# A four-layer decoder trunk on one core: input sums of the FFN spaced out, pairs begin with the unsummed blocks, the norm's matmuls five rounds later

## Chip, core and metric

One core of a Trainium2 chip (trn2). The metric is the device time of one execution in microseconds, here of the one core that runs. Engines: PE is TensorE, DVE is VectorE, ACT is ScalarE, POOL is GpSimd, SP is SyncE, which issues most of the transfers.

## The reference

Four layers on x of shape (1, 512, 1024), each a token mixer and an FFN, both with a norm in front and a residual. All data is float32. The change concerns the FFN:

```python
def rms_norm(x, g):
    return x * rsqrt(mean(x * x, axis=-1) + 1e-6) * g

def conv_ffn(h, w_up, conv_w, conv_b, w_down):      # h: (512, 1024)
    gu = h @ w_up                                   # (512, 5632)
    gate, up = gu[..., :2816], gu[..., 2816:]
    gp = pad(gate, two rows in front)
    conv = conv_b + conv_w[2] * gate + conv_w[0] * gp[0:512] + conv_w[1] * gp[1:513]
    return (silu(conv) * up) @ w_down               # (512, 1024)

for i in range(4):
    x = x + mixer_i(rms_norm(x, norm_mix[i]))
    x = x + conv_ffn(rms_norm(x, norm_ffn[i]), f_w_up[i], f_conv_w[i], f_conv_b[i], f_w_down[i])
```

## The kernel before

**Layout.** x stands transposed: eight tiles x0 to x7 of 128 features by 512 tokens. Every float32 operand of a large product is split in two parts of a shorter type, a high part (written by ACT) and a low part (the rest, written by DVE), and a product is three matmuls: high by high, high by low, low by high (`mm3`, all at L302). A weight tile arrives by DMA as `wraw` or `fraw`, is split into `wh` (ACT, L239) and `wl` (DVE, L242), and there are three buffers of each, so a split is set off when TensorE has finished with an earlier tile (`freew`).

**The end of a mixer.** The output projection of a mixer ends with `x_in` for each of the eight tiles: DVE adds the bank to x (L452), ACT writes `xh`, x times the norm's gain, and the square, DVE writes `xl` (L463) and adds the square to `acc` (L466). When all eight are in, `norm_task` sums `acc` over the partitions with eight small matmuls (`av<-ones,acc`), takes the inverse root on DVE and ACT, and, ahead of an FFN, spreads it with four transposes (L521) and a copy (L523) to `sbc`, which multiplies the FFN's products afterwards.

**The FFN.** 22 blocks of 128 hidden features, each with a gate and an up product. The first two blocks are plain: `plain(0)` and `plain(1)` make gate0, up0, gate1, up1 with 24 matmuls each of 512 columns (`fm`). Their banks are in the rings "a" (three banks) and "lg" (two banks), and are given back when DVE has multiplied them by `sbc` (L670). The other 20 blocks go in ten pairs. A pair is a two by two block product in Winograd's form: seven products of 24 matmuls with 256 columns (`product`) in place of eight. It needs sums of the input's blocks, which `combine(j)` makes once in an FFN from x tiles j and j + 4, for j = 0 to 3: ACT writes y (L623), DVE q1, t3, q2, t4 (L627, L628, L631, L632) into an "r" buffer, ACT splits off `ch` (L293) and DVE `cl` (L295). It also needs sums of the weights' blocks: s1 and s3 come from a load and a second, adding transfer issued by POOL (L256), s2 and s4 from additions on POOL (L220). After a block's two products, `post` does the convolution, the silu, the product with up, and the split into `hh` and `hl` (L646 to L661). The "r" ring has three buffers; `combine`, `plain_post` and the pairs take from it.

**Order.** The program is emitted by generators: TensorE's products are the main line, and after each step of three matmuls of `fm`, or two steps of `product`, a `round` lets every spawned task go on to its next `yield`. What is emitted earlier has the higher priority. A planner in the framework then orders each engine's queue by that priority and by when it expects operands to be ready, and places buffers. On the chip every engine works its queue in order.

Of the kernel before, what the change touches and what calls it, by code (L numbers as in the profile page):

```python
# [25 lines left out]
PARTS = ((0, 4), (4, 8), (8, 12), (12, 16), (16, 22))  # L26

PLAIN = 2
LAM_INIT = 0.8 - 0.6 * math.exp(-0.3 * 2)


# [64 lines left out]
class Builder:  # L96
# [402 lines left out]
    def norm_task(self, bcast):  # L499

        nc = self.nc
        while self.nacc < KD:
            yield
        self.log_exp()
        b = yield from self.take("av")
        for c in range(4):
            self.mm(b[:, 2 * c:2 * c + 2], self.acc[:, c * 128:(c + 1) * 128], self.ones, c == 0, c == 3)
        n = 4
        yield
        u, t, rs, e2 = (self.st[:, 8 * i:8 * i + n] for i in range(4))  # L510
        nc.vector.tensor_scalar(u, b[:, 0:2 * n:2], 1.0 / D, EPS, op0=OP.mult, op1=OP.add)
        self.give("av")
        yield
        yield from self.rsqrt(rs, u, t)
        nc.vector.tensor_scalar(e2, u, EPS, None, op0=OP.mult)
        self.rs, self.e2 = rs, e2
        if bcast:
            yield
            b = yield from self.take("av")
            for c in range(4):  # L520
                nc.tensor.transpose(b[:, c * 128:(c + 1) * 128], rs[:, c:c + 1].to_broadcast([128, 128]), self.ident)  # L521
            yield
            nc.scalar.activation(self.sbc_t, b, AF.Copy)  # L523
            self.give("av")
            self.sbc = self.sbc_t
# [51 lines left out]
    def ffn_weights(self, l):  # L577
        for p, (f0, f1) in enumerate(PARTS):
            downs = 0
            for f in range(f0, f1, 2):  # L580
                t = [self.ap["wup"][(l * NF + f) * 2 + i] for i in range(4)]
                if f < PLAIN:
                    for a in t:
                        self.add_item(self.add_load(a, 1024))
                    continue
                w11 = self.add_load(t[2], 1024)
                s1 = self.add_load(t[0], 1024, "fraw", t[1])
                s2 = self.add_sum(s1, w11)
                s3 = self.add_load(t[0], 1024, "fraw", t[2])
                w12 = self.add_load(t[3], 1024)  # L590
                s4 = self.add_sum(w12, s2)
                w22 = None
                for i, s in enumerate((w11, s1, s2, w12, s3, s4, w22)):
                    self.add_item(s or self.add_load(t[1], 1024))
                    if i in (4, 6) and p and downs < 4:
                        self.add_weights(f"wd{p - 1}", (l * 4 + downs,), 1024)
                        downs += 1
        self.add_weights(f"wd{p}", range(l * KD, (l + 1) * KD), 128 * (f1 - f0))

    def ffn(self, l):  # L600
# [14 lines left out]

        def combine(j):

            while self.xver[j] != stage or self.xver[j + 4] != stage:
                yield
            y = yield from self.take("cv")  # L620
            c = yield from self.take("r")
            c = c.rearrange("p a b -> p (a b)")
            nc.scalar.activation(y, self.x[j], AF.Copy, scale=self.cols[:, gain + j:gain + j + 1])  # L623
            yield
            q1, t3, q2, t4 = (half(c, i) for i in range(4))
            x, k = self.x[j + 4], j + 4
            nc.vector.tensor_tensor(q1, half(y, 0), half(y, 1), op=OP.subtract)  # L627
            nc.vector.scalar_tensor_tensor(t3, half(x, 1), self.cols[:, gain + k:gain + k + 1], half(y, 1), op0=OP.mult,  # L628
                                           op1=OP.subtract)
            yield  # L630
            nc.vector.scalar_tensor_tensor(q2, t3, -1.0, half(y, 0), op0=OP.mult, op1=OP.subtract)  # L631
            nc.vector.scalar_tensor_tensor(t4, half(x, 0), ng[:, k:k + 1], q2, op0=OP.mult, op1=OP.subtract)  # L632
            self.give("cv")
            yield
            h, lo = (fp.tile([128, 1024], F32R, name=f"c{n}{j}") for n in "hl")
            yield from self.split(h, lo, c)
            self.give("r")
            comb[j] = h, lo
# [36 lines left out]
        def plain(f):  # L675
            state = {}
            self.spawn(plain_post(f, state))
            for name, tag in (("gate", "a"), ("up", "lg")):
                w, b = self.getw(), self.now(tag)
                self.fm(b, w, self.xsrc, range(KD))  # L680
                self.freew()
                state[name] = b

        def block(a, b):

            return lambda j: tuple(half(t, b) for t in self.xsrc(j + 4 * a))

        def csrc(i):
            def f(j):
                self.until(lambda: j in comb)  # L690
                return tuple(half(t, i) for t in comb[j])
            return f

        def product(out, src, first=False):

            w = self.getw()
            for j in range(4):
                b = src(j)
                for i in range(2):
                    sl = slice((4 * i + j) * 128, (4 * i + j + 1) * 128)  # L700
                    self.mm3(half(out, i), (w[0][:, sl], w[1][:, sl]), b, first and i + j == 0, True)
                if j % 2:
                    self.round()
            self.freew()
# [6 lines left out]
        def pair(f, downs):  # L711
            st = {}

            def between():
                for _ in range(2):
                    next(downs, None)

            def keep(name, bank):
                st[name] = yield from copied(bank)

            def a_left(bank):
                while "s" not in st:
                    yield
                st["ra"] = yield from self.take("r")
                nc.vector.tensor_tensor(st["ra"][:, :, :256], gu(st["s"]), gu(bank), op=OP.add)
                self.give("a", "cp")

            def a_right(bank):
                while "d" not in st or "ra" not in st:
                    yield  # L730
                nc.vector.tensor_tensor(st["ra"][:, :, 256:], gu(st["d"]), gu(bank), op=OP.add)
                self.give("lg", "cp")
                yield
                yield from scaled(f, st["ra"])

            def b_right(bank):
                while "n" not in st:
                    yield
                st["rb"] = yield from self.take("r")
                nc.vector.scalar_tensor_tensor(st["rb"][:, :, 256:], gu(bank), -1.0, gu(st["n"]), op0=OP.mult,  # L740
                                               op1=OP.subtract)
                self.give("cp")
                st["b"] = True

            def b_left(bank):
                nc.scalar.activation(st["rb"][:, :, :256], gu(bank), AF.Copy, scale=-1.0)
                self.give("a")
                yield
                yield from scaled(f + 1, st["rb"])

            def scaled(f, r):
                nc.vector.tensor_tensor(r, r, self.sbc[:, None, :].to_broadcast([128, 2, S]), op=OP.mult)
                yield
                yield from post(f, r)

            A = self.now("a")
            product(A, block(0, 0), True)
            self.spawn(keep("s", A))
            C = self.now("lg")
            product(C, csrc(0), True)  # L760
            self.spawn(keep("n", C))
            self.until(lambda: "s" in st)
            product(A, csrc(2))
            self.spawn(keep("d", A))
            B = self.now("a")
            product(B, block(1, 0), True)
            self.spawn(a_left(B))
            self.until(lambda: "d" in st)
            product(A, csrc(1))
            self.spawn(b_right(A))  # L770
            between()
            self.until(lambda: "n" in st)
            product(C, block(1, 1))
            self.spawn(a_right(C))
            self.until(lambda: "b" in st)
            product(A, csrc(3))
            self.spawn(b_left(A))
            between()
# [2 lines left out]
            self.until(lambda: f in hid)  # L781
            return hid[f]

        for j in range(4):
            self.spawn(combine(j))
        def downs(f0, f1):

            for _ in self.down_steps(hsrc, range(f0, f1), self.x_add, per=2):
# [3 lines left out]
        d = iter(())  # L792
        for p, (f0, f1) in enumerate(PARTS):
# [7 lines left out]
            d = downs(f0, f1)  # L801
# [1125 lines left out]
```

## Time and profile before

| what | us |
|---|---|
| median of 3 runs | 2389.44 |
| lowest, highest | 2388.29, 2394.17 |
| the profiled execution | 2390.37 |
| its span, first to last instruction | 2388.6 |
| TensorE busy | 2331.5 |
| VectorE busy | 1769.0 |
| ScalarE busy | 1280.5 |
| GpSimd busy | 315.4 |

The profiled execution is 0.9 us above the median, and 1.8 us of it lie outside its span. The mean granted clock of TensorE over the span is 0.991 of full speed. The FFNs' beginnings lie at about 313, 898, 1517 and 2027 us.

### The profile page before, as it was taken

How to read it: one execution, taken by the hardware profiler on the slowest of the kernel's cores; microseconds unless marked ns; L12 is line 12 of the kernel's file. 1: busy time of each engine (PE TensorE's matmuls, PEld its weight loads, DVE VectorE, ACT ScalarE, POOL GpSimd, SP SyncE). 2: the span in 40 equal slices, each digit the busy share in tenths (PEclk: the TensorE clock that was granted, in tenths of full speed). 3: DMA queues.
4: the chain of work that ended last, by engine and by line, in shares of the span. 5: the costliest groups of instructions: out<-in, count | busy, mean ns of one | idle time of the engine just before them, and what ended most of it. 6: DMA issues, size and time to landing. Idle time of an engine off the chain costs nothing.

```text
span 2388.6 us, 41006 instructions
## 1 busy us (share of the span) xinstructions
PE 2331.5 (98%) x16116; PEld 2115.6 (89%) x16116; DVE 1769.0 (74%) x3152; ACT 1280.5 (54%) x2378; POOL 315.4 (13%) x242
## 2 busy tenths in 40 slices
PE   8999989999999999999999998899999999999999
PEld 8999969999997768999989997799999987899998
DVE  6565688787768759877786666798777686987775
ACT  5555555444557756544454554464445575644443
POOL 0000022122002102222100000222220000222220
PEclk9999999999999999999999999999999999999999
DMA  5232255554221126555425454455552442655532
GB/s 181 82 98 89 89 141 164 154 150 133 78 93 45 34 65 173 159 154 151 120 94 159 133 137 113 141 162 150 148 149 76 139 108 91 173 159 158 155 115 84
DMA packets 98160, 298.43 MB, mean 125 GB/s; under 512 B 12144, under 2 KB 18480, under 8 KB 97968
## 3 DMA queue, kind: packets, MB, share of 16 engines
q1 hardware_dynamic: 85296, 249.67, 32.9%
q0 software_dynamic: 12672, 46.14, 11.0%
q8 instruction: 127, 2.08, 0.4%
q14 instruction: 65, 0.53, 0.1%
HBM read 273.62 MB, written 4.32 MB: 116 GB/s over the span
## 4 chain that ended last, share of the span: by engine, by line
PE 93%; DVE 3%; ACT 2%; DMA 1%; issue 1%; SPq 0%; POOL 0%; DVEq 0%; ACTq 0%; POOLq 0%
PE a L302 49%; PE tr L302 19%; PE lg L302 17%; PE av L302 3%; PE tr L961 2%; PE tr L863 2%; DVE r L628 1%; ACT wh L239 0%; DMA sk<-ql 0%; DVE wl L242 0%; DMA sk<-qh 0%; ACT xh L456 0%; DVE acc L466 0%; DMA x<-in_x_dram 0%; DVE xl L463 0%
## 5 line engine op out<-in xcount | busy, mean ns | idle before, releaser
L239 ACT ACTIVATE wh<-wraw 128x1024 fp32r<-128x1024 f32 (+3 forms) x357 | 358.0, 1008 | 493.6 <-PE a L302 216.5
L242 DVE TENSOR_TENSOR wl<-wraw,wh 128x1024 fp32r<-128x1024 f32 (+3 forms) x357 | 441.6, 1239 | 150.9 <-ACT wh L239 149.9
L302 PE MATMUL a<-wh,xh 128*128 128x256 f32 (+1 forms) x1088 | 315.0, 290 | 6.3 <-ACT xh L456 6.3
L302 PE MATMUL a<-wl,xh 128*128 128x256 f32 (+1 forms) x1088 | 311.7, 287 | 0.0
L302 PE MATMUL a<-wh,xl 128*128 128x256 f32 (+1 forms) x1088 | 311.0, 287 | 0.3 <-DVE xl L463 0.3
L302 PE MATMUL a<-ch,wh 128*128 128x256 f32 x960 | 271.7, 283 | 0.0
L302 PE MATMUL a<-cl,wh 128*128 128x256 f32 x960 | 271.5, 283 | 0.0
L302 PE MATMUL a<-ch,wl 128*128 128x256 f32 x960 | 271.4, 283 | 0.0
L302 PE MATMUL tr<-hl,wh 128*128 128x512 f32 x656 | 256.1, 390 | 0.0
L302 PE MATMUL tr<-hh,wh 128*128 128x512 f32 x656 | 255.7, 392 | 0.0
L302 PE MATMUL tr<-hh,wl 128*128 128x512 f32 x656 | 250.5, 390 | 0.0
L256 POOL DMA_DIRECT2D fraw<-in_wup_dram x80 | 69.4, 872 | 1196.0 <-DMA fraw<-in_wup_dram 602.2
L302 PEld LDWEIGHTS a<-wh,xh 128*128 128x128 f32 x1088 | 209.5, 193 | 9.1 <-ACT xh L456 6.3
L302 PEld LDWEIGHTS a<-wl,xh 128*128 128x128 f32 x1088 | 209.6, 193 | 1.5 <-issue 0.4
L302 PEld LDWEIGHTS a<-wh,xl 128*128 128x128 f32 x1088 | 208.7, 192 | 2.2 <-issue 0.9
L302 PE MATMUL a<-xh,wh 128*128 128x256 f32 (+1 forms) x704 | 206.5, 293 | 3.3 <-ACT wh L239 3.3
L302 PE MATMUL a<-xh,wl 128*128 128x256 f32 (+1 forms) x704 | 205.9, 293 | 0.0
L302 PE MATMUL a<-xl,wh 128*128 128x256 f32 (+1 forms) x704 | 204.9, 293 | 0.0
L302 PEld LDWEIGHTS a<-cl,wh 128*128 128x128 f32 x960 | 183.8, 191 | 1.4
L302 PEld LDWEIGHTS a<-ch,wh 128*128 128x128 f32 x960 | 183.7, 191 | 1.4
L302 PEld LDWEIGHTS a<-ch,wl 128*128 128x128 f32 x960 | 183.8, 191 | 0.0
L302 PEld LDWEIGHTS tr<-hh,wl 128*128 128x128 f32 x656 | 123.3, 188 | 25.1
(274 smaller groups left out, 5884.9 us busy)
## 6 DMA issues: line engine op xcount, KB each, us to landing
wraw<-in_wup_dram SPq DMA_DIRECT2D x136, 512.0 KB, 3.3
fraw<-in_wup_dram SPq DMA_DIRECT2D x80, 512.0 KB, 3.4
fraw<-in_wup_dram POOLq DMA_DIRECT2D x80, 512.0 KB, 5.9
wraw<-in_w_dram SPq DMA_DIRECT2D x69, 512.0 KB, 3.4
wraw<-in_wd_dram SPq DMA_DIRECT2D x64, 512.0 KB, 3.4
wraw<-in_wd_dram SPq DMA_DIRECT2D x32, 384.0 KB, 3.0
wraw<-in_o_dram SPq DMA_DIRECT2D x24, 384.0 KB, 3.1
sk<-qh SPq DMA_DIRECT2D x68, 128.0 KB, 2.3
```

The source lines that it names most:

```text
L239: nc.scalar.activation(wh[:, sl], raw[:, sl], AF.Copy)
L242: nc.vector.tensor_tensor(wl[:, sl], raw[:, sl], wh[:, sl].bitcast(F32), op=OP.subtract)
L256: self.nc.gpsimd.dma_start(out=s["tile"][:, :s["n"]], in_=s["plus"], accum_op=OP.add)
L302: self.nc.tensor.matmul(out, a, b, start=start, stop=stop, skip_group_check=True)
L628: nc.vector.scalar_tensor_tensor(t3, half(x, 1), self.cols[:, gain + k:gain + k + 1], half(y, 1), op0=OP.mult, op1=OP.subtract)
L863: self.nc.tensor.transpose(b[:rows, o * 128:(o + 1) * 128], src(c), self.mirror if query else self.ident)
L961: nc.tensor.transpose(tb[i][:, j * 128:(j + 1) * 128], blk, self.mirror)
```

## The change

Four edits. The four `combine` tasks are spawned after the first gate product, not ahead of it, and combine j lets 7 j rounds pass first. In a pair, the second product is now the one of w12 with x tiles 4 to 7 (`block(1, 0)`), and the product of s1 with the combines (`csrc(0)`) comes fourth; the items of the weights, and the load of w12 against that of s3, are put in the same order. Ahead of an FFN, `norm_task` lets five more rounds pass before its matmuls. The arithmetic is the same.

```diff
--- before.py
+++ after.py
@@ -26,6 +26,8 @@
 PARTS = ((0, 4), (4, 8), (8, 12), (12, 16), (16, 22))
 
 PLAIN = 2
+
+COMBINE_GAP, NORM_LATE = 7, 5
 LAM_INIT = 0.8 - 0.6 * math.exp(-0.3 * 2)
 
 
@@ -501,6 +503,8 @@
         nc = self.nc
         while self.nacc < KD:
             yield
+        for _ in range(NORM_LATE if bcast else 0):
+            yield
         self.log_exp()
         b = yield from self.take("av")
         for c in range(4):
@@ -586,11 +590,11 @@
                 w11 = self.add_load(t[2], 1024)
                 s1 = self.add_load(t[0], 1024, "fraw", t[1])
                 s2 = self.add_sum(s1, w11)
+                w12 = self.add_load(t[3], 1024)
                 s3 = self.add_load(t[0], 1024, "fraw", t[2])
-                w12 = self.add_load(t[3], 1024)
                 s4 = self.add_sum(w12, s2)
                 w22 = None
-                for i, s in enumerate((w11, s1, s2, w12, s3, s4, w22)):
+                for i, s in enumerate((w11, w12, s2, s1, s3, s4, w22)):
                     self.add_item(s or self.add_load(t[1], 1024))
                     if i in (4, 6) and p and downs < 4:
                         self.add_weights(f"wd{p - 1}", (l * 4 + downs,), 1024)
@@ -615,6 +619,8 @@
 
         def combine(j):
 
+            for _ in range(COMBINE_GAP * j):
+                yield
             while self.xver[j] != stage or self.xver[j + 4] != stage:
                 yield
             y = yield from self.take("cv")
@@ -680,6 +686,9 @@
                 self.fm(b, w, self.xsrc, range(KD))
                 self.freew()
                 state[name] = b
+                if not f and name == "gate":
+                    for j in range(4):
+                        self.spawn(combine(j))
 
         def block(a, b):
 
@@ -756,15 +765,15 @@
             A = self.now("a")
             product(A, block(0, 0), True)
             self.spawn(keep("s", A))
+            B = self.now("a")
+            product(B, block(1, 0), True)
+            self.spawn(a_left(B))
+            self.until(lambda: "s" in st)
+            product(A, csrc(2))
+            self.spawn(keep("d", A))
             C = self.now("lg")
             product(C, csrc(0), True)
             self.spawn(keep("n", C))
-            self.until(lambda: "s" in st)
-            product(A, csrc(2))
-            self.spawn(keep("d", A))
-            B = self.now("a")
-            product(B, block(1, 0), True)
-            self.spawn(a_left(B))
             self.until(lambda: "d" in st)
             product(A, csrc(1))
             self.spawn(b_right(A))
@@ -781,8 +790,6 @@
             self.until(lambda: f in hid)
             return hid[f]
 
-        for j in range(4):
-            self.spawn(combine(j))
         def downs(f0, f1):
 
             for _ in self.down_steps(hsrc, range(f0, f1), self.x_add, per=2):
```

## Rows read from the trace of the kernel before

**Rows 1.** The page: busy us of each engine (share of the span) and instructions.

```profile
...
PE 2331.5 (98%) x16116; PEld 2115.6 (89%) x16116; DVE 1769.0 (74%) x3152; ACT 1280.5 (54%) x2378; POOL 315.4 (13%) x242
```

**Rows 2.** Stretches: us, busy us of PE, PEld, DVE, ACT, POOL, PEclk, DMA, GB/s.

```profile
...
313.00:357.00 44.00, 36.56 (x180) 30.63 (x180) 39.91 (x60) 24.26 (x35) 14.34 (x8) 0.92 0.68 178
898.00:941.00 43.00, 38.11 (x200) 32.74 (x199) 39.65 (x59) 25.27 (x36) 11.96 (x8) 0.92 0.70 184
1517.00:1558.00 41.00, 34.21 (x177) 29.26 (x176) 37.34 (x56) 22.37 (x33) 14.62 (x8) 0.92 0.70 187
2027.00:2069.00 42.00, 36.74 (x185) 31.20 (x184) 37.69 (x56) 23.12 (x33) 12.19 (x8) 0.92 0.69 180
...
960.00:1220.00 260.00, 260.00 (x1825) 244.51 (x1824) 207.47 (x220) 126.50 (x160) 52.05 (x30) 1.00 0.51 140
...
924.40:931.45 7.05, 6.98 (x23) 5.60 (x24) 4.81 (x12) 1.47 (x3) 0.00 (x0) 0.72 0.70 223
889.70:899.20 9.50, 9.50 (x43) 7.82 (x42) 8.09 (x11) 6.33 (x10) 0.00 (x0) 1.00 0.30 105
```

**Rows 3.** TensorE's timeline: start, duration, instruction [idle before <- releaser].

```profile
...
339.65 1.84 PE L302 MATMUL av<-ones,acc 128*128 128x2 f32 x8 [5.06 <-DVE acc L466]
...
924.47 0.80 PE L302 MATMUL lg<-xh,wl 128*128 128x512 f32 x1 [4.45 <-DVE wl L242]
...
931.43 0.28 PE L302 MATMUL a<-xh,wl 128*128 128x256 f32 x1
...
1542.56 0.79 PE L302 MATMUL lg<-xh,wl 128*128 128x512 f32 x1 [5.76 <-DVE wl L242]
...
2053.27 0.80 PE L302 MATMUL lg<-xh,wl 128*128 128x512 f32 x1 [4.23 <-DVE wl L242]
```

**Rows 4.** Timelines of ACT, POOL and DVE, second FFN's beginning.

```profile
...
917.10 2.01 ACT L239 ACTIVATE wh<-wraw 128x1024 fp32r<-128x1024 f32 x2 [0.64 <-PE a L302]
...
916.89 2.83 POOL L220 TENSOR_TENSOR ws<-fraw,wraw 128x1024 f32<-128x1024 f32 x1 [4.30 <-DMA fraw<-in_wup_dram]
919.79 2.40 POOL L220 TENSOR_TENSOR ws<-wraw,ws 128x1024 f32<-128x1024 f32 x1
...
914.18 0.68 DVE L466 TENSOR_TENSOR acc<-acc,sq 128x512 f32<-128x512 f32 x1
...
917.38 2.61 DVE L628 SCALAR_TENSOR_TENSOR r<-x,cols,cv 128x256 f32<-128x256 f32 x1
919.92 3.35 DVE L295 TENSOR_TENSOR cl<-r,ch 128x1024 fp32r<-128x1024 f32 x1
923.20 1.21 DVE L242 TENSOR_TENSOR wl<-wraw,wh 128x1024 fp32r<-128x1024 f32 x1
```

**Rows 5.** DVE groups, 905 to 942 us: busy, mean ns of one, idle before.

```profile
...
L295 DVE TENSOR_TENSOR cl<-r,ch 128x1024 fp32r<-128x1024 f32 x4 | 6.9, 1754 | 0.6 <-ACT ch L293 0.6
L242 DVE TENSOR_TENSOR wl<-wraw,wh 128x1024 fp32r<-128x1024 f32 x4 | 4.9, 1236 | 0.0
L628 DVE SCALAR_TENSOR_TENSOR r<-x,cols,cv 128x256 f32<-128x256 f32 x4 | 4.1, 1013 | 0.0
...
L632 DVE SCALAR_TENSOR_TENSOR r<-x,ng,r 128x256 f32<-128x256 f32 x4 | 1.7, 476 | 0.0
L627 DVE TENSOR_TENSOR r<-cv 128x256 f32<-128x256 f32 x4 | 1.7, 418 | 0.0
```

**Rows 6.** The chain that ended last, 930 to 965 us: start, us, what.

```profile
...
949.71 5.76 PE a L302 x48
```

**Rows 7.** POOL and ACT timelines in the middle of the second FFN.

```profile
...
1037.18 2.40 POOL L220 TENSOR_TENSOR ws<-wraw,ws 128x1024 f32<-128x1024 f32 x1 [4.65 <-DMA wraw<-in_wup_dram]
...
1041.42 1.05 ACT L239 ACTIVATE wh<-fraw 128x1024 fp32r<-128x1024 f32 x1
```

**Rows 8.** DVE timeline: the first gate multiply and the first post's last operation.

```profile
...
933.70 0.68 DVE L670 TENSOR_TENSOR r<-a,acc 128x512 f32<-128x512 f32 x1
...
944.25 0.69 DVE L295 TENSOR_TENSOR hl<-r,hh 128x512 fp32r<-128x512 f32 x1
```

## Prediction

> **What bounds the kernel now.** I read the page's engine line first. TensorE is busy for 2331.5 of 2388.6 us [rows 1], so at most 57 us of waiting can be won, and the question is whether any of it lies where the diff acts. The table of stretches answers that. In the middle of an FFN, 960 to 1220 us, TensorE is busy for all 260 us [rows 2]. In the four beginnings it is not: 44 − 36.56 = 7.4, 43 − 38.11 = 4.9, 41 − 34.21 = 6.8 and 42 − 36.74 = 5.3 us, together 24.4 us of idle time. In the same four stretches the DVE (VectorE) is busy for 37 to 40 of 41 to 44 us. So the pairs are bound by TensorE, and the beginnings by VectorE with TensorE behind it.
>
> TensorE's own timeline then names the waits. One long wait in each beginning makes up 5.06 + 4.45 + 5.76 + 4.23 = 19.5 of the 24.4 us [rows 3]; the other 4.9 us are waits of about 1 us or less. Three of the long ones wait for a wl of L242, the low half of a weight tile. The first waits for acc, which the norm's matmuls read. Each costs more than its length. After the one at 924 us the granted clock is 0.72 in the mean, part of the stretch at the 1.2 GHz level, and 23 matmuls take 7.05 us; where it is 1.00 (2.4 GHz), 43 of that shape take 9.50 us, 0.22 each [rows 2]. The 22 that follow the wait would take 4.9 us, so some 2.0 us more are lost. The pattern stands four times, so the beginnings waste about 24.4 + 8 = 32 us.
>
> Why is wl late? In the second beginning its high half wh is written on ScalarE from 917.10 us, two tiles in 2.01 us, so the first is there at about 918.1. VectorE starts wl at 923.20 [rows 4]. Ahead of it in its queue stand operations of the fourth combine and of the third: L628 (2.61 us) and a cl (3.35 us). Both are stretched. The four L628 take 4.1 us together, so the other three take 0.5 each; the four cl take 6.9, so the other three 1.2 [rows 5]. What runs beside the stretched ones is the first two weight sums on POOL, 2.83 and 2.40 us [rows 4]. The sums thus cost VectorE about 2.1 + 2.1 = 4.3 us, and it is the combines, which nobody needs yet, that pay in front of the wl that TensorE waits for.
>
> **The change, part by part.** No arithmetic is added or removed. *Spaced combines:* they are now issued after the first gate product and 7 rounds apart, a round being one step of three matmuls in the plain products. The split of the fourth tile (the last up product) is set off when that gate product frees its buffers, so before the first combine. Its wl therefore no longer stands behind L628 and cl. That takes away the long wait, 19.5 us, and its clock, 8 us.
>
> *Unsummed blocks first:* the second product of a pair now reads x blocks 4 to 7 and the plain tile w12, where it read combine results and the tile s1, which a second load adds to. The first use of a combine moves from the second product to the third. A product is 24 matmuls at 5.76/48 = 0.12 us [rows 6], so the combines get 2.9 us more.
>
> *The later norm:* five rounds are 15 matmuls at 0.22, 3.3 us later in the order. In the first FFN it was the norm's matmuls that held TensorE for 5.06 us; with other products ahead of them the wait for acc is covered. What is late next is the broadcast scale, its four gate and up multiplies (L670), and the bank that the second product of the first pair takes, which the first multiply gives back. Without the three combines' small operations (3 × (0.42 + 0.48 + 0.42 + 0.48) = 5.4 us of durations, some 4.4 by spacing, since each start comes about 0.07 before the end ahead) acc is ready at about 910.4, not 914.8 [rows 4, 5]. The two shifts nearly cancel, so I cost the five rounds at nothing; if the cover fails, the bank wait is at most their 3.3 us a beginning.
>
> *What the VectorE ledger leaves.* Second beginning, from 910.4 us: combines 4.1 + 6.9 + 1.7 + 1.7 and a last set like L627, 1.7 (blocked time included), 16.1; four wl at 1.24, 4.9; four multiplies at 0.68 [rows 8], 2.7; small norm operations, an estimate, 0.8. That is 24.5 us of durations, about 22.3 by spacing: 932.7, and with the post operations of f = 0 (four, the last one 0.69 [rows 8]) ahead, up to 935.5. TensorE, without its 4.45 + 2.0 us, ends the plain products, where the first pair's first matmul (128x256) starts, at 931.43 − 6.5 = 924.9 [rows 3], the next two products at 930.7, and wants the last combine 18 matmuls later, at 932.9. So VectorE is level with demand: the new wait is 0 to 2.6 us. I take 2 us, and 1 us a beginning for small waits that stay: 3 × 4 = 12 us. Waits so short I cost without a drop of the clock; the bound with the drop is the first rival.
>
> *The pairs' order in the steady state.* 40 pairs reorder loads, splits and products. The load of w12 moves ahead of that of s3 on SP's queue, and so ahead of s3's adding transfer on POOL's. The tile w12 is split two items sooner, in the place that the next pair's s1 had, 1041.42 us on ScalarE. The sum that reads w12 had already started at 1037.18 [rows 7], so the tile has landed 4 us before it is wanted. Between A's copies there is still one whole product (2.9 us) each time. Cost nothing; if that cover went, 1 us a pair would be 40 us, the upper bound of the loss.
>
> Sum: 32 − 12 = 20 us. The profiled execution took 2390.4 us (span 2388.6 and 1.8 around it), so 2370.4; the runs' median lies 0.9 below it, so 2369.5, forecast **2369 us**.
>
> **A rule against it.** The rows show that sums and two-input VectorE operations stretch one another, whichever operation it is [rows 4, 5]. The Trainium skill, "SBUF — State Buffer", section "SBUF: two separate sides", says that VectorE operations with two SBUF inputs and GpSimd operations hold the shared ports in turn, each for a whole instruction, and the other side blocks fully. By that rule the lock isn't spared but falls on whatever VectorE then runs, wl too, and the gain is that of the second rival below, 10 us in place of 20. The trace agrees as far as a combine's operations go: 2.61 for 0.5 and 3.35 for 1.2 us. Whether wl stands there when the sums run depends on the new order, which no row shows.
>
> **The rivals.** *The debt moves.* VectorE is behind in the third product instead: the 4.3 us of blocked time plus the post operations come ahead of the last combine, a 3.5 us wait and 2 us of clock each. 32 − 4 × 5.5 = 10 us gained: 2379. For it speaks the level ledger; against it, the ledger counts all four multiplies and the post operations, and only the first two multiplies free banks that the third and fourth products need.
>
> *The sums hit wl.* If wl is at the head when both sums run (916.89 to 922.19), it ends at about 923.4 and TensorE, out of work at 924.47 − 4.45 = 920.0 [rows 3], waits 3.4 us, clock 2 us: 32 − 22 = 10 us gained, 2379. Against it: without the combines the gate product ends sooner, and wl may be done before 916.89.
>
> *A buffer makes it slower.* The combine takes one of three r buffers, and post takes them too. If the third combine is handed the buffer of f = 0's post, it waits for that chain: 11.2 us from L670 at 933.70 to the end of hl at 944.94 [rows 8]. L670, freed of 6.5 us, would come at 927.2, hl at 938.4, the third combine's cl about 3.9 us later (its small operations 1.5, two splits of 1.2) at 942.3, wanted at 932.1: 10.2 us and 2 of clock, four times, is 49 against 32: 17 us slower, 2406. It decides once that L670 comes after about 923. Against it: two combines have given back their buffers by then.
>
> *It does nothing.* The emitted order is only a priority; the planner may still place combines ahead of wl, the long waits stay: 2389.
>
> **How the numbers follow.** Forecast 0.58, debt 0.14, sums on wl 0.08, no effect 0.12, buffer 0.08. The forecast's own ends are 32 us (all won) and 12 us. The two rivals with a gain of 10 reach to 2379, or a few us further if the small waits grow too. The range 2358 to 2384 holds the first three cases, 0.80. A measurement of this kernel tells about 0.3%, 7 us, from no change: faster 0.80, same 0.12, slower 0.08.
>
> **What would show it.** Right: in each beginning the DVE order has the fourth wl before the last combines, TensorE has no wait over 3 us there, the granted clock is near 1.00 in them, the four stretches lose under 12 us together, and the pairs' 260 us stay full. Wrong in part: a wait for cl or r in front of the third product, or a wl that lasts over 2 us beside a sum. Wrong altogether: waits inside the later pairs, the same 4 to 6 us waits for wl, or a combine that stands behind L295's hl.

## The result: slower by 24 us, and the profile after

The median is 2412.55 us (2412.07 to 2413.98) beside 2388.86 us for the kernel before: ratio 1.0092 [1.0079, 1.0104]. The profiled execution's span is 2412.2 us, 23.6 more than before.

Where it went is read from the first plain matmul of an FFN to the first down product, in TensorE's timeline:

| FFN | before, us | after, us | difference |
|---|---|---|---|
| first | 65.96 | 68.53 | +2.6 |
| second | 64.73 | 72.39 | +7.7 |
| third | 63.88 | 69.67 | +5.8 |
| fourth | 65.69 | 73.12 | +7.4 |

Together 23.5 us, the whole loss. From there to the end of the FFN's last down product both kernels take 290.8 us each time. The page's engine line and the table of stretches after (us, busy us of PE, PEld, DVE, ACT, POOL, PEclk, DMA, GB/s):

```profile
PE 2346.9 (97%) x16116; PEld 2128.2 (88%) x16116; DVE 1763.9 (73%) x3152; ACT 1283.3 (53%) x2378; POOL 311.0 (13%) x242
```

```profile
313.00:371.00 58.00, 49.21 (x272) 43.02 (x271) 51.51 (x72) 33.19 (x47) 15.64 (x10) 0.91 0.62 160
898.00:958.00 60.00, 51.06 (x265) 44.12 (x264) 53.17 (x71) 33.45 (x48) 15.95 (x10) 0.89 0.58 157
1517.00:1583.00 66.00, 57.28 (x284) 49.39 (x285) 54.81 (x77) 35.30 (x49) 15.64 (x10) 0.84 0.53 139
2032.00:2105.00 73.00, 64.50 (x336) 56.23 (x335) 61.64 (x79) 38.00 (x51) 16.86 (x10) 0.91 0.54 150
...
936.00:940.00 4.00, 0.74 (x4) 0.53 (x4) 3.83 (x6) 3.08 (x4) 0.00 (x0) 0.86 0.38 131
940.00:949.00 9.00, 5.50 (x24) 4.70 (x24) 8.81 (x16) 3.96 (x6) 1.72 (x2) 0.68 0.86 176
949.00:958.00 9.00, 7.46 (x39) 6.87 (x40) 6.67 (x5) 4.28 (x7) 2.38 (x1) 0.62 0.01 2
958.00:968.00 10.00, 10.00 (x86) 10.00 (x85) 9.09 (x11) 6.47 (x9) 0.00 (x0) 1.00 0.46 159
...
980.00:1240.00 260.00, 260.00 (x1802) 243.61 (x1801) 200.19 (x221) 126.77 (x162) 49.80 (x28) 1.00 0.48 136
```

TensorE runs the same 16116 matmuls in 15.4 us more than in [rows 1], and is idle for 2412.2 − 2346.9 = 65.3 us in place of 57.1. The mean granted clock fell from 0.991 to 0.984. From the first plain matmul to the first down product alone, the four together, it is 249.7 − 235.9 = 13.8 us more of busy time and 34.0 − 24.4 = 9.6 us more of waiting. So some three fifths of the loss are matmuls at a lower clock, and the rest is waiting. The idle time of the beginnings in the windows of this table, 8.8 + 8.9 + 8.7 + 8.5 = 34.9 us, lies later than in [rows 2]: no longer in the plain products but in the first pair. The middle of the pairs is full.

What TensorE waits for there (the view of waits, TensorE: total, times, longest), and the second beginning's waits in its timeline:

```profile
PE a L304 <- ACT ch L295: 19.6, 8, 3.2
...
PE a L304 <- DVE cl L297: 8.4, 10, 1.7
...
PE lg L304 <- DVE wl L244: 4.3, 4, 1.8
```

```profile
937.16 0.38 PE L304 MATMUL lg<-ch,wl 128*128 128x256 f32 x1 [1.79 <-DVE wl L244]
...
940.76 0.58 PE L304 MATMUL a<-ch,wh 128*128 128x256 f32 x1 [2.87 <-ACT ch L295]
...
942.07 0.58 PE L304 MATMUL a<-cl,wh 128*128 128x256 f32 x1 [0.51 <-DVE cl L297]
...
949.66 0.58 PE L304 MATMUL a<-ch,wh 128*128 128x256 f32 x1 [2.88 <-ACT ch L295]
```

The four long waits of [rows 3] are gone; what is left of the waits for `wl` is at most 1.8 us long. In their place TensorE waits for the combines' results, two long times in each beginning for `ch`, and shorter for `cl` behind it. The lines moved by two to six: L302 is L304, L242 is L244, L295's `cl` is L297, L627 is L633, L670 is L676. The `ch` waits are the combines too: ScalarE splits `ch` off the r buffer that VectorE fills. So VectorE's and ScalarE's queues say why (same beginning):

```profile
915.87 1.23 DVE L297 TENSOR_TENSOR cl<-r,ch 128x1024 fp32r<-128x1024 f32 x1 [0.52 <-ACT ch L295]
919.34 4.54 DVE L244 TENSOR_TENSOR wl<-wraw,wh 128x1024 fp32r<-128x1024 f32 x2 [2.24 <-ACT wh L241]
923.80 0.15 DVE L515 TENSOR_SCALAR st<-av 128x4 f32<-128x4 f32 x1
923.99 2.18 DVE L519 TENSOR_SCALAR st<-st 128x4 f32<-128x4 f32 x1
...
928.88 0.69 DVE L676 TENSOR_TENSOR r<-a,acc 128x512 f32<-128x512 f32 x1 [1.08 <-ACT acc L527]
929.49 0.68 DVE L676 TENSOR_TENSOR r<-lg,acc 128x512 f32<-128x512 f32 x1
930.08 0.42 DVE L633 TENSOR_TENSOR r<-cv 128x256 f32<-128x256 f32 x1
...
932.61 2.62 DVE L637 SCALAR_TENSOR_TENSOR r<-r,cv 128x256 f32<-128x256 f32 x1
935.16 0.41 DVE L633 TENSOR_TENSOR r<-cv 128x256 f32<-128x256 f32 x1
...
940.80 1.22 DVE L297 TENSOR_TENSOR cl<-r,ch 128x1024 fp32r<-128x1024 f32 x1
941.94 0.68 DVE L297 TENSOR_TENSOR hl<-r,hh 128x512 fp32r<-128x512 f32 x1
...
943.74 1.22 DVE L297 TENSOR_TENSOR cl<-r,ch 128x1024 fp32r<-128x1024 f32 x1
944.87 0.42 DVE L633 TENSOR_TENSOR r<-cv 128x256 f32<-128x256 f32 x1
...
949.64 1.23 DVE L297 TENSOR_TENSOR cl<-r,ch 128x1024 fp32r<-128x1024 f32 x1 [0.25 <-ACT ch L295]
```

```profile
908.49 1.32 ACT L629 ACTIVATE cv<-x,cols 128x512 f32<-128x512 f32 x2
```

Only the first combine's `cl` (915.87) stands ahead of the gate multiply (L676, 928.88). The second combine's y was written with the first's by 909.81, yet its first operation on VectorE comes at 930.08, right behind the gate and the up multiply, although VectorE stood idle for 2.24 and 1.08 us in between. The third follows at 935.16, the fourth at 944.87, behind the post of f = 0 (`hl` at 941.94). The gate multiply itself came 26.2 us after the first plain matmul (902.63), where it was 34.5 in the kernel before (933.70 in [rows 8] less 899.22). But the last `cl` ends 48.2 us after that first matmul, and 30.6 in the kernel before, which had all four ahead of the multiply. The last of them there:

```profile
928.61 1.22 DVE L295 TENSOR_TENSOR cl<-r,ch 128x1024 fp32r<-128x1024 f32 x1 [0.59 <-ACT ch L293]
```

### The profile page after: what moved, and what is told of

It reads as the page before. It is cut to its first block, busy times and chain, and to the rows that moved or that the text cites. A ratio compares the mean times of both kernels' runs of the same rounds, so it can differ in the third digit from the quotient of the medians.

```text
span 2412.2 us, 41043 instructions
## 1 busy us (share of the span) xinstructions
PE 2346.9 (97%) x16116; PEld 2128.2 (88%) x16116; DVE 1763.9 (73%) x3152; ACT 1283.3 (53%) x2378; POOL 311.0 (13%) x242
## 4 chain that ended last, share of the span: by engine, by line
PE 93%; DVE 4%; ACT 1%; DMA 1%; issue 1%; SPq 0%; ACTq 0%; DVEq 0%
PE a L304 50%; PE tr L304 19%; PE lg L304 16%; PE av L304 3%; PE tr L968 2%; PE tr L870 2%; DVE cl L297 1%; DMA sk<-ql 0%; DVE wl L244 0%; DVE r L637 0%; DMA sk<-qh 0%; DVE r L676 0%; DVE r L633 0%; ACT wh L241 0%; DVE cv L656 0%
## 5 line engine op out<-in xcount | busy, mean ns | idle before, releaser
L244 DVE TENSOR_TENSOR wl<-wraw,wh 128x1024 fp32r<-128x1024 f32 (+3 forms) x357 | 441.8, 1241 | 157.8 <-ACT wh L241 154.6
L304 PE MATMUL a<-wh,xh 128*128 128x256 f32 (+1 forms) x1088 | 315.0, 290 | 5.8 <-ACT xh L458 5.8
L304 PE MATMUL a<-wl,xh 128*128 128x256 f32 (+1 forms) x1088 | 311.8, 287 | 0.0
L304 PE MATMUL a<-wh,xl 128*128 128x256 f32 (+1 forms) x1088 | 311.0, 287 | 0.0
L304 PE MATMUL a<-ch,wh 128*128 128x256 f32 x960 | 278.2, 290 | 21.3 <-ACT ch L295 19.6
L304 PE MATMUL a<-cl,wh 128*128 128x256 f32 x960 | 278.0, 290 | 8.4 <-DVE cl L297 8.4
L304 PE MATMUL a<-ch,wl 128*128 128x256 f32 x960 | 276.0, 288 | 0.0
L304 PE MATMUL tr<-hl,wh 128*128 128x512 f32 x656 | 256.2, 390 | 0.0
L304 PE MATMUL tr<-hh,wh 128*128 128x512 f32 x656 | 255.6, 392 | 0.0
L304 PE MATMUL tr<-hh,wl 128*128 128x512 f32 x656 | 250.4, 390 | 0.0
L304 PEld LDWEIGHTS a<-wh,xh 128*128 128x128 f32 x1088 | 209.6, 193 | 8.7 <-ACT xh L458 5.8
L304 PEld LDWEIGHTS a<-ch,wh 128*128 128x128 f32 x960 | 188.6, 196 | 25.7 <-ACT ch L295 21.4
L304 PEld LDWEIGHTS a<-wl,xh 128*128 128x128 f32 x1088 | 209.7, 193 | 1.5 <-issue 0.4
L304 PEld LDWEIGHTS a<-wh,xl 128*128 128x128 f32 x1088 | 208.9, 193 | 1.7 <-issue 0.9
L304 PE MATMUL a<-xh,wl 128*128 128x256 f32 (+1 forms) x704 | 206.1, 293 | 0.0
L304 PE MATMUL a<-xh,wh 128*128 128x256 f32 (+1 forms) x704 | 206.0, 293 | 0.0
L304 PE MATMUL a<-xl,wh 128*128 128x256 f32 (+1 forms) x704 | 205.2, 293 | 0.0
L304 PEld LDWEIGHTS a<-cl,wh 128*128 128x128 f32 x960 | 188.6, 196 | 13.1 <-DVE cl L297 11.6
L304 PEld LDWEIGHTS a<-ch,wl 128*128 128x128 f32 x960 | 188.9, 197 | 0.0
L304 PEld LDWEIGHTS tr<-hh,wl 128*128 128x128 f32 x656 | 123.3, 188 | 25.1
```

The costliest lines, as they stand in the source:

```text
L244: nc.vector.tensor_tensor(wl[:, sl], raw[:, sl], wh[:, sl].bitcast(F32), op=OP.subtract)
L304: self.nc.tensor.matmul(out, a, b, start=start, stop=stop, skip_group_check=True)
```

## The experiments

The theory formed from that: a combine that is emitted after `plain_post` of f = 0 has asked for its buffer is given its own after it. The planner hands out a ring's buffers ("r", and "cv" for y) in the order of emission, so the later combines are placed behind the multiply, which waits for the norm's whole chain, and in part behind the posts. Rivals: the pairs' new order, the number of buffers, and the spacing itself, with the posts' work coming between.

**The spacing undone.** Spawn and gap go back; pairs and norm stay as changed.

```diff
-            for _ in range(COMBINE_GAP * j):
-                yield
...
-                if not f and name == "gate":
-                    for j in range(4):
-                        self.spawn(combine(j))
...
+        for j in range(4):
+            self.spawn(combine(j))
```

> The combines are spawned where they were before the change; the pairs' new order and the later norm stay. Theory A (the spacing costs: a combine that is emitted after the first block's gate multiply gets its r buffer after it, so it runs behind the norm): the loss is gone, 2380 to 2392 us. Theory B (the later norm costs) or C (the pairs' order costs): most of the 24 us stays, 2400 to 2412 us.

2389.82 us, ratio 0.9998 [0.9988, 1.0007]. The loss lies in the moved combines, and the waits for `wl` are back (4.46, 5.95 and 4.23 us).

**The pairs' order alone**, in the kernel before.

```diff
-                for i, s in enumerate((w11, s1, s2, w12, s3, s4, w22)):
+                for i, s in enumerate((w11, w12, s2, s1, s3, s4, w22)):
...
-            C = self.now("lg")
-            product(C, csrc(0), True)
-            self.spawn(keep("n", C))
+            B = self.now("a")
+            product(B, block(1, 0), True)
+            self.spawn(a_left(B))
```

> The kernel before with the pairs' new order alone (norm and combines as before). All theories that put the loss on the combines' spacing: 2386 to 2392 us, no change. Theory C: 2395 us or more. The first forecast had the first use of a combine 2.9 us later; as the long wait for wl stands ahead of it, that gains under 4 us in all.

2389.7 us, 0.9999 [0.999, 1.0008]. By itself it neither gains nor loses.

**The combines not spaced**, spawned after the gate product all the same.

```diff
-COMBINE_GAP, NORM_LATE = 7, 5
+COMBINE_GAP, NORM_LATE = 0, 5
```

> The combines are still spawned after the first gate product, but with no rounds between them. Theory A: the first three are emitted ahead of the gate multiply and take their buffers before it, only the fourth comes behind: most of the loss is gone, 2380 to 2395 us. Theory D (VectorE has too much work there in whatever order, because the sums block it): 2400 us or more.

2394.94 us, 1.002 [1.001, 1.0029]. Three combines now stand ahead of the multiply, the fourth behind, and 18 us of the loss are gone.

**The norm at once.**

```diff
-COMBINE_GAP, NORM_LATE = 7, 5
+COMBINE_GAP, NORM_LATE = 7, 0
```

> The norm's matmuls lose their five rounds, spacing and pairs stay as changed. Theory B: the loss goes, about 2390 us. Theory A: the gate multiply is emitted earlier still, so even the first combine falls behind it: 2405 to 2420 us.

2415.79 us, 1.0109 [1.0093, 1.0126]. Now even the first combine stands behind the multiply (fourth beginning: L676 at 2070.55, the first L633 at 2071.16). The loss is all there, and the intervals of this run and the change overlap. So the five rounds were not what hurt; they had kept one combine ahead.

**The norm 24 rounds late**: as changed, but the last spaced combine (21 rounds) is emitted first.

```diff
-COMBINE_GAP, NORM_LATE = 7, 5
+COMBINE_GAP, NORM_LATE = 7, 24
```

> The changed kernel with one number altered: the norm waits 24 rounds in place of 5. The combines keep their gaps of 7 rounds and their rings; they are now all emitted ahead of the gate multiply. If the order against the gate multiply is the whole cause: 2385 to 2393 us, the loss of 24 us is gone. If spacing has a cost of its own: 2396 us or more.

2388.73 us, 0.9993 [0.9984, 1.0002]: one number takes the whole loss away, with the spacing left in. VectorE's timeline, second beginning, has all four `cl` ahead of the multiplies (L676), and again two combines' stretched operations ahead of `wl`, as in [rows 4]:

```profile
914.64 2.35 DVE L297 TENSOR_TENSOR cl<-r,ch 128x1024 fp32r<-128x1024 f32 x2
...
917.24 2.61 DVE L634 SCALAR_TENSOR_TENSOR r<-x,cols,cv 128x256 f32<-128x256 f32 x1
919.78 3.35 DVE L297 TENSOR_TENSOR cl<-r,ch 128x1024 fp32r<-128x1024 f32 x1
923.06 1.21 DVE L244 TENSOR_TENSOR wl<-wraw,wh 128x1024 fp32r<-128x1024 f32 x1
...
928.46 1.23 DVE L297 TENSOR_TENSOR cl<-r,ch 128x1024 fp32r<-128x1024 f32 x1 [0.58 <-ACT ch L295]
...
934.05 1.29 DVE L676 TENSOR_TENSOR r<-a,acc 128x512 f32<-128x512 f32 x2
```

So the emission of the combines, late in the program text or spaced, doesn't by itself move them behind `wl`. It moves them only when something else is handed a buffer in between.

**Gap 3, norm 12 rounds late.** The same test with 9 rounds of spacing.

```diff
-COMBINE_GAP, NORM_LATE = 7, 5
+COMBINE_GAP, NORM_LATE = 3, 12
```

> Spaced combines still, 3 rounds apart, and the norm 12 rounds later in place of 5, so that all four combines are emitted ahead of the gate multiply; rings as in the change. Theory A: no loss, 2384 to 2393 us, as with the combines in their old place. Theory B (the later norm costs): slower than the changed kernel, 2415 us or more. If spacing as such costs: 2400 us or more.

2390.06 us, 1.0 [0.9991, 1.0009]. No loss and no gain, as above.

**Four r buffers**, with one `cp` buffer fewer to make room.

```diff
-("r", [128, 2, S], F32, 3), ("cv", [128, S], F32, 3), ("cp", [128, S], F32, 3),
+("r", [128, 2, S], F32, 4), ("cv", [128, S], F32, 3), ("cp", [128, S], F32, 2),
```

> The changed kernel with four r buffers in place of three (and two cp in place of three). Theory A, order of emission: the second combine still stands behind the gate multiply although a buffer is free: 2405 to 2414 us. Theory E (there are too few buffers, a combine waits until a post gives one back): at least half of the loss goes, 2385 to 2400 us.

2414.47 us, 1.0099 [1.0082, 1.0117]. VectorE, second beginning:

```profile
931.16 0.69 DVE L676 TENSOR_TENSOR r<-a,acc 128x512 f32<-128x512 f32 x1 [1.08 <-ACT acc L527]
...
932.37 0.41 DVE L633 TENSOR_TENSOR r<-cv 128x256 f32<-128x256 f32 x1
```

The second combine still starts right behind the multiplies. The number of buffers isn't it, which leaves the order in which they are handed out.

**A ring of their own**: the combines take from "rc", one buffer, which `post` doesn't touch. As above, one `cp` buffer fewer makes room.

```diff
+                                     ("rc", [128, 2, S], F32, 1),
...
-            c = yield from self.take("r")
+            c = yield from self.take("rc")
...
-            self.give("r")
+            self.give("rc")
```

> The combines take a ring of their own (one buffer), paid for with one of the three cp buffers; all else as changed. Theory A: the second combine no longer waits for the gate multiply, at least a third of the loss goes: 2385 to 2404 us. Theories B, C and D: no change, 2408 to 2416 us.

2409.28 us, 1.0078 [1.0063, 1.0093]: at most some 3 us came back, with an interval that overlaps the change's, and fewer than the theory of the ring had led me to expect. VectorE, second beginning (L634 opens a combine, L677 is the multiply here):

```profile
914.22 0.41 DVE L634 TENSOR_TENSOR rc<-cv 128x256 f32<-128x256 f32 x1
...
920.02 0.43 DVE L634 TENSOR_TENSOR rc<-cv 128x256 f32<-128x256 f32 x1
...
933.62 0.69 DVE L677 TENSOR_TENSOR r<-a,acc 128x512 f32<-128x512 f32 x1
...
938.12 0.41 DVE L634 TENSOR_TENSOR rc<-cv 128x256 f32<-128x256 f32 x1
...
946.28 0.42 DVE L634 TENSOR_TENSOR rc<-cv 128x256 f32<-128x256 f32 x1
```

The second combine has moved ahead of the multiply, from 930.08 to 920.02, so the r ring held that one: its place in the order of emission is as before, and one `cp` buffer fewer did not move it in the run above. The third and fourth still stand behind. Their y is taken from "cv", and the convolution of `post` takes from that ring too.

**Their own ring, and y from another.** As above, with y from the ring of the norm's squares.

```diff
-            y = yield from self.take("cv")
-            c = yield from self.take("r")
+            y = yield from self.take("sq")
+            c = yield from self.take("rc")
```

> As the run with the combines' own ring, and their y is taken from the ring of the squares, which stands idle then, in place of the cv ring that post takes from too. Theory A (buffers of a ring are handed out in the order of emission, and a combine behind a post's take waits for the gate multiply) in its second form, both rings count: combines 0 to 2 come ahead of the gate multiply, only the fourth behind it: at least half of the loss goes, 2380 to 2400 us. Theory D (VectorE has too much work there, whatever the order): 2403 us or more.

2410.43 us, 1.0087 [1.0074, 1.01]: no better in time. Three combines now start ahead of the multiply, so both rings held them. But a single buffer runs them one after another, the multiply comes behind what the third has started, and TensorE waits for the bank that the multiply gives back:

```profile
PE a L304 <- DVE r L677: 15.3, 4, 5.1
PE a L304 <- ACT ch L295: 13.9, 4, 4.0
```

The fourth combine still starts behind the four multiplies of the two posts, and in the first and third beginnings its `cl` comes behind both `hl`. This run mixes the cure with a new wait and shows the order, not its worth. No run has a second "rc" buffer.

**y from the other ring alone**, in the changed kernel and in the kernel before.

```diff
-            y = yield from self.take("cv")
+            y = yield from self.take("sq")
```

> The changed kernel with y from the squares' ring alone; norm 5 rounds late as in the change. The r buffers still come behind the gate multiply: 2404 to 2416 us. If the y ring were the cause of the later gains: 2390 us or less.

> The kernel before, with one edit: the combines' y is taken from the squares' ring in place of the cv ring. If the gain of the run with y from that ring, no gaps and the norm 8 rounds late comes from the ring (the combines' first operations then come behind the last squares, so x's own operations go first): 2376 to 2386 us. If it comes from the wl that is moved ahead of the combines: 2387 to 2393 us.

2412.92 us, 1.0088 [1.007, 1.0107] on the change: nothing, since the r ring holds the combines first. On the kernel before 2384.92 us, 0.9978 [0.9969, 0.9987], 5 us gained.

**The posts wait for the combines.** `plain_post` goes on behind its multiplies only when all four combines are emitted.

```diff
+            while len(comb) < 4:
+                yield
             yield from post(f, r)
```

> The changed kernel, but each plain block's post (convolution, silu, split) is emitted only when all four combines have been; the gate and up multiplies stay where they are. Theory F (what costs is the posts' VectorE work in front of the last combine): half of the loss or more goes, 2388 to 2402 us. Theory A (the wait for the gate multiply costs): the second combine still stands behind it, 2403 to 2412 us.

2405.82 us, 1.0065 [1.0051, 1.0079]. The posts' operations between the combines cost about 7 us of the loss. The other 17 are still there with the combines behind the multiply alone.

**Versions that combine it.** Gap 0, norm 8 rounds late, y from "sq"; then gap 7, norm 24 rounds late, y from "sq"; then this last one with the pairs' old order. The edit of the second:

```diff
-COMBINE_GAP, NORM_LATE = 7, 5
+COMBINE_GAP, NORM_LATE = 7, 24
...
-            y = yield from self.take("cv")
+            y = yield from self.take("sq")
```

> The combines without gaps after the first gate product, y from the ring of the squares, the norm 8 rounds late: all combines ahead of the gate multiplies, and the last up product's wl ahead of most of the combines' work. Theory A with the first forecast's account of the waits (wl behind the combines costs 32 us): 2365 to 2384 us, faster than before. Theory D: about 2390 us, the waits only move.

> The spacing of the change (7 rounds), y from the squares' ring, and the norm 24 rounds late, so that all four combines are emitted, and take their buffers, ahead of the gate multiply. Theories A and F: as fast as the run without gaps, 2372 to 2384 us. If spacing as such costs: 2390 us or more.

> The fastest version so far (gaps of 7, norm 24 rounds late, y from the squares' ring) with the pairs' old order. If the new order of the pairs matters once the combines are on time: 2381 to 2390 us, slower than 2378. If it does not: 2375 to 2381 us.

2379.86 us, 0.9956 [0.9943, 0.9968]; **2377.93 us, 0.995 [0.9937, 0.9962]**, faster than both kernels; and 2384.27 us, 0.9973 [0.9963, 0.9983]. With the combines in time, the pairs' new order is worth about 6 us. In the best one, the second, the last `cl` comes at 927.83, ahead of the multiplies, and only 1.4 us of waits for `wl` are left. VectorE's second beginning and TensorE's waits:

```profile
912.75 1.23 DVE L244 TENSOR_TENSOR wl<-wraw,wh 128x1024 fp32r<-128x1024 f32 x1 [0.58 <-ACT wh L241]
...
914.31 1.23 DVE L297 TENSOR_TENSOR cl<-r,ch 128x1024 fp32r<-128x1024 f32 x1
...
922.14 2.34 DVE L244 TENSOR_TENSOR wl<-wraw,wh 128x1024 fp32r<-128x1024 f32 x2
...
927.83 1.22 DVE L297 TENSOR_TENSOR cl<-r,ch 128x1024 fp32r<-128x1024 f32 x1
...
932.27 1.27 DVE L676 TENSOR_TENSOR r<-a,acc 128x512 f32<-128x512 f32 x2
```

```profile
PE av L525 <- DVE st L326: 8.0, 4, 3.7
...
PE a L304 <- DVE wl L244: 1.4, 2, 0.9
```

What is late next is the norm's scale (`st`, 8.0 us in four waits). Some 12 of the beginnings' 32 us are won. No run takes apart why y's other ring brings so much on top of the late norm (2388.73 to 2377.93), but the two traces show what it moves. With y from "sq" the first combine starts only behind the last addition to `acc` (907.66), and the `wl` of the last up product runs at 912.75, 16.0 us after the first plain matmul (896.72). In the run with the norm 24 rounds late and y from "cv", three combines start ahead of that addition (914.03), the same `wl` runs at 923.06, 24.0 us after (899.08), and TensorE waits 4.45 us for it.

## Why the prediction was wrong, step by step

**Right: the long waits, and the pairs.** *Spaced combines* does take the 4 to 6 us waits for `wl` and `acc` away; none is left. *The pairs' order in the steady state* costs nothing: 260 of 260 us full, and 2389.7 us alone.

**The failed step: *What the VectorE ledger leaves*.** It let VectorE work from `acc` on without a gap, the combines first, and found it level with demand: a last `cl` at 33.5 to 36.3 us after the first plain matmul and a wait of 0 to 2.6 us. The last `cl` ended at 48.2 us. Combines two to four do not start when VectorE is free: they stand behind the gate multiply and so behind the norm's chain, because the buffers of "r" and "cv" are handed out in the order of emission. With the order the sum was wrong too. Between the end of `acc` (915.34) and that of the last `cl` VectorE stands idle for some 4.5 us, and six `wl` and most of both posts' operations come ahead, where the ledger had four `wl` and one post. One number that changes the order of emission takes the loss away (norm 24 rounds late, 2388.73) or leaves all of it (norm at once, 2415.79). The rings' part in the order is shown by the two runs with other rings, which move combines ahead one by one; neither shows what that is worth. The prediction had named the sign: a combine that stands behind `hl`, as the fourth does (944.87 behind 941.94).

**The second: "waits so short I cost without a drop of the clock".** Where 12 us of waits were predicted, 34.9 came, and the matmuls besides took 15.4 us longer than before, where the forecast gave back 8 us. Working for the second beginning: 8.9 us idle and, at a granted clock of 0.68 and 0.62, 24 matmuls in 5.50 and 39 in 7.46 us where 0.12 each would do (2.6 and 2.8 more), 14.3 in all. Before it was 4.9 + 2.0; the difference of 7.4 is close to the 7.7 measured.

***The later norm*, costed at nothing**, was right to be no loss, but for another reason. It decided how many spaced combines were handed a buffer before `plain_post`: none at 0 rounds, one at 5, four at 24.

***Unsummed blocks first*** put the first use of a combine later, as said. That is worth nothing while the combines are early (2389.7) and about 6 us when the best version uses it.

**The rivals.** *A buffer makes it slower* named the place, the sign and nearly the size (2406 beside 2412.55), and its condition was met: the gate multiply came at 928.88, after the 923 that it gave. Its account of the buffers was off: it had two combines through first and the third waiting for `post` to give its buffer back, but the second already stands behind the multiply, and a fourth buffer changes nothing. *The sums hit wl* is seen too: two `wl` take 4.54 us at 919.34 in place of 2.4. It delays the norm's chain, but with the norm 24 rounds late the sums stretch combines as before (2.61 and 3.35 us) and the loss is gone, so the order is the greater part. *The debt moves* named the wait that came, for a combine in the pair's third product, at 3.5 + 2 us a beginning in place of the second beginning's 8.9 + 5.4. *It does nothing* is what the change gives with the norm 24 rounds late: then the order is that of before.

## What to carry to other kernels

Where a planner hands out shared buffers in the order of emission, as here, moving a task later in the program also moves it behind whoever asks for the same ring in between, and behind all that this taker waits for; before costing such a move, list the takers of each ring in the new order. Sum a queue's work only after fixing its order. And a cluster of short waits should be priced with its clock: here the slower matmuls cost 13.8 us more and the waiting 9.6.

## What was not expected of the hardware

In the second beginning after the change, single waits of 1.79, 2.87, 0.51 and 2.88 us between 935 and 950 us, with four, two and 22 matmuls between them, were followed by a granted clock of 0.68 and 0.62 in the mean over 940 to 949 and 949 to 958 us. Part of it was at the 1.2 GHz level, where matmuls of 256 columns follow one another in 0.21 us in place of 0.12 (942.45 and 942.67). It was 1.00 again from 958 us, with TensorE full. Before, the one wait of 4.45 us was followed by 0.72 over 7 us [rows 2]. So in this beginning the several waits, 8.9 us together, cost 5.4 us in slower matmuls, or 0.6 for each us of waiting, and the single one before cost 2.0 for 4.45 us, or 0.45. Two cases make no rule.

Even a tiny operation is held up by a sum on POOL: L519, 128x4, takes 2.18 us at 923.99 and ends as the sum beside it does, and it takes 0.15 us in the best version, where no sum runs beside it. L515 at 923.80, which reads a bank of PSUM, takes 0.15 us beside the same sum. The sum after the change, then L519 in the best version:

```profile
922.87 3.26 POOL L222 TENSOR_TENSOR ws<-wraw,ws 128x1024 f32<-128x1024 f32 x1
```

```profile
924.74 0.15 DVE L519 TENSOR_SCALAR st<-st 128x4 f32<-128x4 f32 x1
```

The Trainium skill, "SBUF — State Buffer", section "SBUF: two separate sides", says that the ports shared by the two engines are locked for a whole instruction, on VectorE's side by an operation with two SBUF inputs or in a two-port mode. The trace agrees for `wl`, which has two inputs (4.54 us for two at 919.34, 2.34 at 922.14 in the best version); L519 has one, and no row shows its mode.
